# Two state-space chains that start one piece of the output projection later, in a Hymba-style decoder step on one core

## The chip, the cores and the metric

The kernel runs on one core of a Trainium2 chip. The metric is the device time of one execution in microseconds (us); lower is better. Engine names: PE is TensorE (matmuls), DVE VectorE, ACT ScalarE, POOL GpSimd, SP SyncE, which here only issues transfers.

## The reference

One inference step of one layer: sliding-window attention and a Mamba-2 state-space mixer side by side, an output projection, a squared-ReLU MLP. There are 1024 prompt tokens with 16 meta tokens ahead of them, and 32 sample tokens of 8 running sequences. The part that matters here, cut:

```python
def ssd_scan(x, dt, a, bm, cm, h0, chunk):            # chunks of 128 tokens, 8 heads
    ...
    decay = jnp.exp(jnp.where(causal, seg, -jnp.inf))
    g = jnp.einsum('bcthn,bcshn->bctsh', ch, bh) * decay
    y_diag = jnp.einsum('bctsh,bcshp->bcthp', g, xdt)
    s_chunk = jnp.einsum('bclhn,bclh,bclhp->bchpn', bh, to_end, xdt)
    ...
    def step(h, inp):                                 # the state goes from chunk to chunk
        s_c, tot_c = inp
        return h * tot_c[:, :, None, None] + s_c, h
    ...
    y_off = jnp.einsum('bclhn,bchpn->bclhp', ch, h_in) * jnp.exp(acum)[..., None]

def mix_and_mlp(h, ao, so, attn_out_g, w_out, norm2_g, w_up, w_down):
    mix = jnp.concatenate([rmsnorm(ao, attn_out_g), so], axis=-1)
    h = h + mix @ w_out
    u = jax.nn.relu(rmsnorm(h, norm2_g) @ w_up)
    return h + (u * u) @ w_down
```

## The kernel before, in words

The tokens are cut into nine state-space tiles: tile 0 has the 32 sample tokens and the 16 meta tokens, tiles 1 to 8 have 128 prompt tokens each. In the stage of this text two kinds of work share the engines.

The first is the attention half of the output projection, `wout_stream`. It has 24 pieces, one for an output block m of 128 rows and a token chunk ch: (0,0), (0,1), (1,0), (1,1), (0,2), (1,2), and then (m,0), (m,1), (m,2) for m from 2 to 7. A piece loads its rows of x (`hb<-in_xm`, L1013, two pieces ahead, four buffers), runs 12 matmuls into a bank g of three (288 or 384 columns, each product as three matmuls of high and low parts), adds the bank on DVE (`hb<-hb,g`, L1027) and stores the sum (`hd<-hb`, L1028, on SP).

The second is the state-space work, a chain for each tile, `mixer(i)`, which runs `ssd(i)` and then `gate(i)`; a generator whose `yield`s cut it into portions. Portion by portion, with the names of the tiles:

- PE transposes the tile's x (`s<-cs,xs`, L1081) and B (`s<-cs,bc`, L1083) and forms C·B (`s<-bc`); ACT scales x (L1087) and copies B (`Bt`, L1095); DVE makes `xd` (L1092) and `Gm` (L1097), POOL `xw` (L1094).
- PE makes the exponents of the decay in two halves (`s<-R,L`), ACT turns each into `Mt` (L1106, then L1107), DVE multiplies by `Gm` (L1108).
- After two more portions: `y<-Mt,xd`, the state's new part `s<-xw,Bt`, the state `hn` (POOL L1121 scales the last tile's, DVE L1126 adds; tile 0's is a plain ACT copy, L1128), and for tiles from 1 on `f<-bc,hn`; DVE adds the parts up (L1135 to L1138).
- Tile 0 goes on with four sample-state steps, `sample_state(j)`: each loads two tiles of 512 KB through SP (`st`, L1160, and `sT`, L1162), multiplies `sT` (`s<-sT,bc`), transposes the result (L1189), scales `st` on ACT (L1199), adds `s<-Bm,xS` to it on DVE (L1203) and stores it.
- `gate(i)` loads `zt` (L1212) and norms and splits the tile's output for the second half of the projection.

The banks of PSUM named s are a ring of three, shared by all chains; y and f have one each. `factors(i)` loads the decay factors `eA` (L967, two transfers) two slots ahead of the chain. `exponents` writes `R` and `L` for four tiles together.

`interleave` sets the order in which the program is written: slot by slot, first the chains that are due join, each live chain gives one portion, and then the stream gives one piece.

```python
            while chains and (chains[0][0] <= slot or not (more or live)):
                live.append(chains.pop(0)[1])
            live = [g for g in live if next(g, 1) is None]
            if more:
                more = next(gemms, 1) is None
            slot += 1
```

The slots are `round(2.25 * i)`, with 12 for tile 5: 0, 2, 4, 7, 9, 12, 14, 16, 18 for the tiles 0 to 8. From the written order the framework's scheduler makes the order on each engine, so that an instruction can stand some places away from where it is written; on each engine, SP's queue too, instructions then start in that order.

Of the kernel before, what the change touches and what calls it, by code (L numbers as in the profile page):

```python
# [20 lines left out]
NT = 9  # L21
# [167 lines left out]
def body(ctx: ExitStack, tc: tile.TileContext, xT, xm, win, wdt, wo, wu, wd, ck, cv, sc, st, sT, vec, consts,  # L189
# [5 lines left out]
    def pool(name, bufs=1, **kw):  # L195
        return tc.tile_pool(name=name, bufs=bufs, reuse_waits="tile", **kw)
# [13 lines left out]
    def gps():  # L210
        return psg.tile([128, 512], F32, name="g", tag="g", bufs=3)
# [32 lines left out]
    class Ahead:  # L244
# [9 lines left out]
        def next(self):  # L254
            while self.fns and len(self.got) <= self.n:
                self.more()
            return self.got.pop(0)

    def gemm(ps, w, act, k0=0):

        halves = isinstance(w[0], list)
        nk = 8 if halves else w[0].shape[1]
        for k in range(nk):
            for n, (a, b) in enumerate(((0, 0), (0, 1), (1, 0))):
                mm(ps, w[a][k // 4][:, k % 4, :] if halves else w[a][:, k, :], act[b][(k0 + k) // 4][:, (k0 + k) % 4, :], k == 0 and n == 0, k == nk - 1 and n == 2)

    def interleave(gemms, chains):

        gemms, chains, slot, live = iter(gemms), sorted(chains, key=lambda x: x[0]), 0, []
        more = True  # L270
        while more or live or chains:
# [6 lines that stand above are left out]
# [682 lines left out]
    def factors(i):  # L960

        M = TOK[i][1]
        z = "0" if i == 0 else ""
        eA = sp.tile([128, 4, M], F32, name="eA", tag="eA" + z, bufs=1 if i == 0 else 3)
        for hh in range(2):
            src = ed[8 * i:8 * i + 8, 0:M].rearrange("(j q) t -> q j t", q=2)[hh]
            SP.dma_start(out=eA[HALF[hh]], in_=src.unsqueeze(0).broadcast_to([64, 4, M]))  # L967
        EA[i] = eA
        yield
# [9 lines left out]
    def load_kept(m, ch, wk):  # L979

        c0, cw = CM[ch]
        hb = wk.tile([128, 384], F32, name="hb", tag="hb", bufs=4)[:, :cw]
        SP.dma_start(out=hb, in_=hd[:, m, c0:c0 + cw])
        return hb

    def mixer_half(m, ch, w, hb, wk, eng, tag="s2"):

        c0, cw = CM[ch]
        ps = gps()
        gemm(ps[:, :cw], w, X[ch], 4)  # L990
        DVE.tensor_tensor(out=hb, in0=hb, in1=ps[:, :cw], op=ALU.add)
        if m == 0:
            ACT.activation(out=sq[ch], in_=hb, func=AF.Square)
        else:
            s2 = wk.tile([128, 384], F32, name="s2", tag=tag, bufs=1 if tag == "s2" else 4)
            ACT.activation(out=s2[:, :cw], in_=hb, func=AF.Square)
            eng.tensor_tensor(out=sq[ch], in0=sq[ch], in1=s2[:, :cw], op=ALU.add)

    def gained(m, out, x):

        ACT.activation(out=out, in_=x, func=AF.Copy, scale=vec[:, V_G2 + m:V_G2 + m + 1])
# [3 lines left out]
    def wout_stream():  # L1005

        ws, hbs = {}, []
        order = [(0, 0), (0, 1), (1, 0), (1, 1), (0, 2), (1, 2)] + [(m, ch) for m in range(2, 8) for ch in range(3)]

        def load_x(m, ch):  # L1010
            c0, cw = CM[ch]
            hb = sp.tile([128, 384], F32, name="hb", tag="hb", bufs=4)[:, :cw]
            SP.dma_start(out=hb, in_=xm[:, 8 * c0 + m * cw:8 * c0 + (m + 1) * cw])  # L1013
            hbs.append(hb)

        load_x(*order[0])
        load_x(*order[1])
        for n, (m, ch) in enumerate(order):
            c0, cw = CM[ch]
            if m not in ws:  # L1020
                ws[m] = weights.next()
            if n + 2 < len(order):
                load_x(*order[n + 2])
            hb = hbs.pop(0)
            ps = gps()
            gemm(ps[:, :cw], ws[m], X[ch])
            DVE.tensor_tensor(out=hb, in0=hb, in1=ps[:, :cw], op=ALU.add)  # L1027
            SP.dma_start(out=hd[:, m, c0:c0 + cw], in_=hb)  # L1028
            yield
        acta_s.close()  # L1030
        opb = act_s.enter_context(pool("opb", side="right"))

        ha = xn["ha"] = opb.tile([128, 8, TM], F32, name="ha")
        c2 = CM[2][0]
        first = [load_kept(0, ch, sp) for ch in range(2)]
        SP.dma_start(out=ha[:, 1], in_=hd[:, 1])
        SP.dma_start(out=ha[:, 2], in_=hd[:, 2])
        SP.dma_start(out=ha[:, 0, c2:], in_=hd[:, 0, c2:])
        for m in range(3, 8):
            SP.dma_start(out=ha[:, m], in_=hd[:, m])  # L1040
        sq01 = opb.tile([128, CM[2][0]], F32, name="sq01")
        sq.update({ch: sq01[:, CM[ch][0]:CM[ch + 1][0]] for ch in range(2)})
        pieces = [(m, ch) for m in range(8) for ch in range(2)]
        weights.n = 3
        for m, ch in pieces:
            c0, cw = CM[ch]
            if ch == 0:
                w = weights.next()
            hb = ha[:, m, c0:c0 + cw] if m else first[ch]
            mixer_half(m, ch, w, hb, sp, DVE if m > 2 else POOL)  # L1050
            if m == 0:
                SP.dma_start(out=he[:, m, c0:c0 + cw], in_=hb)
                gained(m, ha[:, m, c0:c0 + cw], hb)
            elif ch == 0 and m > 1:
                SP.dma_start(out=he[:, m - 1, 0:c2], in_=ha[:, m - 1, 0:c2])
            elif ch == 1 and m > 3:
                gained(m - 3, ha[:, m - 3, 0:c2], ha[:, m - 3, 0:c2])
            yield
        SP.dma_start(out=he[:, 7, 0:c2], in_=ha[:, 7, 0:c2])
        for m in (5, 6, 7):  # L1060
            gained(m, ha[:, m, 0:c2], ha[:, m, 0:c2])
# [163 lines left out]
    def decays(i):  # L1225
        exponents(*((48, 32, slice(0, 1)) if i == 0 else (128, 128, slice(i, i + 4))))
        yield

    def mixer(i):
        if i == 0:  # L1230
            yield from decays(i)
        yield from ssd(i)

    interleave(wout_stream(), [(max(0, (12 if i == 5 else round(2.25 * i)) - 2), factors(i)) for i in range(NT)] + [(12 if i == 5 else round(2.25 * i), mixer(i)) for i in range(NT)] +
               [(1, decays(1)), (10, decays(5))])
    SP.dma_start(out=hp, in_=hs[8])
    w3.close()
# [656 lines left out]
```

## Time and profile before

| | us |
|---|---|
| median of 3 runs | 1120.18 |
| the three runs | 1119.13 to 1121.18 |
| the profiled execution | 1119.52 |
| its span, first to last instruction | 1117.8 |
| mean granted clock of TensorE over the span | 0.997 of full speed |
| the stage of the two kinds of work | about 290 to 394 of the span |

A row of the timeline gives start, duration, engine, line, operation, output<-input, shape and count; several like instructions in a row are merged, and what stands in brackets is the idle time before and what ended it. A row of the waits gives who waited for whom, the sum in us, how often, and the longest. A row of windows gives the window, its length, the busy time of each engine shown, TensorE's granted clock, the share of the transfer engines and GB/s. All matmuls are issued from L199. (i) behind a name in the text is the tile's number, counted from 0.

### The profile page before, as it was taken

To read this page: it belongs to the slowest core of one execution; us is meant where nothing else is said; L and a number is where in the kernel's file an instruction comes from. 1 tells how busy PE (TensorE), PEld (TensorE's weight loads), DVE (VectorE), ACT (ScalarE), POOL (GpSimd) and SP (SyncE) were. 2 spreads that over 40 slices of the span, in tenths; PEclk is the share of its full clock that TensorE was granted. 3 is DMA by queue.
4 is the path that set the end of the run, shared out by engine and by line. 5 is a ranking of instruction groups with operands and counts; after the bars stand their busy time and mean duration, and the time that the engine had idled before them with its cause. 6 is when DMAs were issued, how large, how long until landed. Compare 5 with 4: busy or idle time off the path is not lost.

```text
span 1117.8 us, 21656 instructions
## 1 busy us (share of the span) xinstructions
PE 1101.4 (99%) x8312; PEld 1063.4 (95%) x8312; DVE 832.7 (75%) x1652; ACT 557.3 (50%) x1188; POOL 215.4 (19%) x296
## 2 busy tenths in 40 slices
PE   9999999999999999999999999999999999999997
PEld 8989988989888899999999999999999999999997
DVE  6646888985879968988877777676599657768483
ACT  8312467575655558744444444444434343546461
POOL 0442365564245432200000000000000000000001
PEclk9999999999999999999999999999999999999999
DMA  8231110111497486656643434425989663465273
GB/s 285 73 99 39 40 37 22 39 59 53 140 273 235 142 290 223 207 183 229 200 150 139 179 106 157 161 100 203 392 291 311 190 182 90 127 197 161 80 230 110
DMA packets 89259, 179.53 MB, mean 161 GB/s; under 512 B 11488, under 2 KB 37704, under 8 KB 87108
## 3 DMA queue, kind: packets, MB, share of 16 engines
q1 hardware_dynamic: 82372, 143.76, 41.2%
q0 software_dynamic: 6080, 33.48, 7.5%
q8 instruction: 65, 1.06, 0.4%
q10 hardware_dynamic: 704, 0.92, 0.2%
q14 instruction: 38, 0.31, 0.1%
HBM read 127.36 MB, written 50.76 MB: 159 GB/s over the span
## 4 chain that ended last, share of the span: by engine, by line
PE 78%; DVE 10%; issue 4%; ACT 3%; POOL 3%; DMA 2%; POOLq 0%; SPq 0%; DVEq 0%; ACTq 0%
PE g L199 44%; PE b L199 18%; PE c L199 9%; PE s L199 3%; PE o L199 1%; DVE bc L522 1%; DMA wdr<-in_wd 1%; POOL wlo L231 1%; PE y L199 1%; DVE Sd L1639 1%; PE pt L199 1%; DMA wraw<-in_win 1%; DVE p L675 1%; DMA u<-b 1%; DVE ts L1653 0%
## 5 line engine op out<-in xcount | busy, mean ns | idle before, releaser
L199 PE MATMUL g<-acth,whi 128*128 128x384 f32 (+2 forms) x528 | 161.4, 331 | 0.2 <-DVE qT L452 0.2
L199 PE MATMUL g<-acth,wlo 128*128 128x384 f32 (+2 forms) x528 | 159.8, 327 | 0.0
L199 PE MATMUL g<-actl,whi 128*128 128x384 f32 (+2 forms) x432 | 140.4, 325 | 0.0
L1652 ACT CAST ts<-tr 128x528 fp32r<-128x528 f32 x92 | 58.2, 632 | 119.1 <-PE b L199 97.4
L1653 DVE TENSOR_TENSOR ts<-tr,ts 128x528 fp32r<-128x528 f32 x92 | 65.1, 708 | 56.6 <-ACT ts L1652 56.1
L199 PEld LDWEIGHTS g<-acth,whi 128*128 128x128 f32 x528 | 97.0, 188 | 2.1 <-issue 1.2
L199 PEld LDWEIGHTS g<-acth,wlo 128*128 128x128 f32 x528 | 97.6, 189 | 0.5 <-issue 0.2
L199 PEld LDWEIGHTS g<-actl,whi 128*128 128x128 f32 x432 | 81.4, 188 | 0.2
L318 POOL TENSOR_TENSOR rs<-rs,nhalf 128x3 f32<-128x3 f32 x9 | 9.6, 1066 | 338.7 <-DVE rs L317 338.7
L1368 ACT COPY s<-g 128x264 f32<-128x264 f32 x90 | 34.0, 377 | 63.7 <-PE g L199 61.7
L231 POOL TENSOR_TENSOR wlo<-wraw,whi 128x256 fp32r<-128x256 f32 x56 | 48.9, 903 | 10.9 <-ACT whi L228 10.6
L1441 POOL DMA_DIRECT2D u<-u x16 | 8.5, 532 | 177.2 <-ACT u L1384 146.7
L1373 DVE TENSOR_TENSOR u<-b,s 128x264 f32<-128x264 f32 x64 | 27.5, 430 | 19.7 <-PE b L199 10.1
L1378 ACT ACTIVATE u<-u 128x528 f32<-128x528 f32 x42 | 27.1, 646 | 26.6 <-DVE u L1377 26.6
L199 PE MATMUL b<-ts,w7y 128*128 128x264 f32 x279 | 39.3, 285 | 0.0
L199 PE MATMUL g<-ts,whi 128*128 128x264 f32 x279 | 38.9, 284 | 0.0
L199 PE MATMUL g<-ts,w7y 128*128 128x264 f32 x279 | 38.9, 283 | 0.0
L199 PE MATMUL b<-ts,whi 128*128 128x264 f32 x279 | 38.9, 284 | 0.0
L199 PE MATMUL g<-ts,wlo 128*128 128x264 f32 x270 | 38.0, 285 | 0.0
L199 PE MATMUL b<-ts,wlo 128*128 128x264 f32 x270 | 37.3, 283 | 0.0
L199 PEld LDWEIGHTS b<-ts,w7y 128*128 128x128 f32 x279 | 36.1, 188 | 0.0
L199 PEld LDWEIGHTS b<-ts,whi 128*128 128x128 f32 x279 | 36.0, 188 | 0.0
(588 smaller groups left out, 3430.1 us busy)
## 6 DMA issues: line engine op xcount, KB each, us to landing
tr<-u SPq DMA_DIRECT2D x92, 264.0 KB, 3.0
wraw<-in_wu SPq DMA_DIRECT2D x38, 512.0 KB, 4.0
wdr<-in_wd SPq DMA_DIRECT2D x68, 256.0 KB, 3.6
u<-t POOLq DMA_DIRECT2D x16, 1056.0 KB, 5.7
wraw<-in_win SPq DMA_DIRECT2D x16, 512.0 KB, 3.7
u<-u POOLq DMA_DIRECT2D x10, 792.0 KB, 3.6
wraw<-in_wo SPq DMA_DIRECT2D x24, 256.0 KB, 2.8
h<-he SPq DMA_DIRECT2D x16, 264.0 KB, 5.3
```

The lines of the kernel that those rows point to most:

```text
L199: PE.matmul(out, lhsT=a, rhs=b, start=start, stop=stop, skip_group_check=on)
L231: eng.tensor_tensor(out=lo[:, n], in0=raw[:, n], in1=f(hi[:, n]), op=ALU.subtract)
L318: POOL.tensor_tensor(out=out, in0=out, in1=nhalf[:out.shape[0], :w], op=ALU.pow)
L522: DVE.scalar_tensor_tensor(out=acc, in0=cb[:, j:j + CL], scalar=cw_(j), in1=acc, op0=ALU.mult, op1=ALU.add)
L675: DVE.tensor_tensor_reduce(out=s_out[:, 0:W], in0=ps, in1=mask, scale=-scale, scalar=nsink, op0=ALU.add, op1=ALU.min, accum_out=nm)
L1368: ACT.copy(out=s[:, c], in_=ps[c][:, :TQ])
L1373: DVE.tensor_tensor(out=out[:, c], in0=ps[c][:, :TQ], in1=s[:, c], op=ALU.add)
L1378: ACT.activation(out=x, in_=x, func=AF.Square)
L1441: POOL.dma_start(out=u7[p][:, 4 + a:7], in_=u[:, a:3])
L1639: tt(out=s, in0=s, in1=r, op=ALU.subtract)
L1652: ACT.copy(out=t[:, 0], in_=x)
L1653: DVE.tensor_tensor(out=t[:, 1], in0=x, in1=f(t[:, 0]), op=ALU.subtract)
```

## The change

The slot of each chain comes from a small function, which gives 3 for tile 1 (before 2), 5 for tile 2 (before 4), and the same as before for all others. The loads of the decay factors of those two tiles start one slot later as well (1 and 3 for 0 and 2).

```diff
-    interleave(wout_stream(), [(max(0, (12 if i == 5 else round(2.25 * i)) - 2), factors(i)) for i in range(NT)] + [(12 if i == 5 else round(2.25 * i), mixer(i)) for i in range(NT)] +
+    def at_slot(i):
+        return {1: 3, 2: 5, 5: 12}.get(i, round(2.25 * i))
+
+    interleave(wout_stream(), [(max(0, at_slot(i) - 2), factors(i)) for i in range(NT)] + [(at_slot(i), mixer(i)) for i in range(NT)] +
                [(1, decays(1)), (10, decays(5))])
```

The number of instructions is the same; the order on the engines differs from the first pieces of the stream to the end of the stage. Three places follow. Numbers behind a name tell buffers apart, and differ between the two kernels.

SP's queue around the first sample-state step, before. hb_3257, hb_3259, hb_3271, hb_3323, hb_3381 and hb_3409 belong to the pieces (0,0), (0,1), (1,0), (1,1), (0,2) and (1,2):

```order
L1028 DMA hd_3227<-hb_3259 128x384
L1160 DMA st_3490<-in_st 128x1024
L1013 DMA hb_3381<-in_xm 128x384
L1028 DMA hd_3227<-hb_3271 128x288
L1013 DMA hb_3409<-in_xm 128x384
L1028 DMA hd_3227<-hb_3323 128x384
L1162 DMA sT_3492<-in_sT 128x1024
```

And after; here the same six pieces are hb_3254, hb_3256, hb_3268, hb_3323, hb_3356 and hb_3398, and hb_3449 is piece (2,0):

```order
L1028 DMA hd_3227<-hb_3268 128x288
L1013 DMA hb_3398<-in_xm 128x384
L1028 DMA hd_3227<-hb_3323 128x384
L1160 DMA st_3468<-in_st 128x1024
L1013 DMA hb_3449<-in_xm 128x288
L1028 DMA hd_3227<-hb_3356 128x384
L1162 DMA sT_3470<-in_sT 128x1024
```

The issue of sT stood behind the store of piece (1,1), and now stands behind the store of piece (0,2), one piece later.

DVE's queue at the same place, before (Mt_3398 is tile 1's; g_3383 and g_3411 are the banks of the pieces (1,0) and (1,1)):

```order
L1097 TENSOR_TENSOR Gm_3371<-s_3355,cs_66 128x256
L1027 TENSOR_TENSOR hb_3271<-hb_3271,g_3383 128x288
L1108 TENSOR_TENSOR Mt_3398<-Mt_3398,Gm_3371 128x512 x2
L1027 TENSOR_TENSOR hb_3323<-hb_3323,g_3411 128x384
L1136 TENSOR_TENSOR xs0_3236<-xs0_3236,y_3426 128x192
```

And after (Mt_3438 is tile 1's, xd_3489 is tile 2's; g_3451 is the bank of piece (0,2)):

```order
L1146 TENSOR_TENSOR xS_3430<-xw_3300,xS_3430 32x512
L1146 TENSOR_TENSOR BS_3431<-Bt_3301,BS_3431 32x256
L1108 TENSOR_TENSOR Mt_3438<-Mt_3438,Gm_3393 128x512 x2
L1027 TENSOR_TENSOR hb_3356<-hb_3356,g_3451 128x384
L1092 TENSOR_TENSOR xd_3489<-s_3475,dt_111 128x512
```

The sum of piece (0,2), which SP's store waits for, now stands directly behind the Mt pair of tile 1. On ACT the four steps that make this pair stand behind tile 0's copy, after:

```order
L1145 CAST xS_3430<-xw_3300 32x512
L1128 COPY hn_3425<-s_3424 128x512
L1106 ACTIVATE Mt_3438<-s_3439 128x512
L1106 ACTIVATE Mt_3438<-s_3444 128x512
L1107 ACTIVATE Mt_3438<-Mt_3438 128x512 x2
```

Before, they stood ahead of that copy.

PE at the first sample-state step, as one piece of the difference (- before, + after; the sT row is the step; acth_3099 belongs to piece (1,2), acth_3091 to piece (2,0); y, f and s<-xw,Bt are tile 1's, s<-R,L tile 2's):

```order
 L199 MATMUL g<-acth_3099,wlo 128x384
-L199 MATMUL s<-sT,bc_3237 32x128 x8
+L199 MATMUL y<-Mt,xd 64x128 x8
+L199 MATMUL f<-bc,hn 128x128 x4
 L199 MATMUL g<-acth_3091,whi 128x288
 L199 MATMUL g<-actl_3093,whi 128x288
-L199 MATMUL g<-acth_3091,whi 128x288 x2
+L199 MATMUL g<-acth_3091,whi 128x288
+L199 MATMUL s<-sT,bc_3237 32x128 x8
+L199 MATMUL s<-xw,Bt 128x256 x2
+L199 MATMUL s<-R,L 128x512 x2
+L199 MATMUL g<-acth_3091,whi 128x288
```

The multiplication by sT stood between the pieces (1,2) and (2,0). It now stands behind the first three matmuls of piece (2,0), and tile 1's s<-xw,Bt and tile 2's two decay matmuls stand behind it.

## The prediction

> **What bounds the kernel now.** I read the busy times and the chain of the page first, then the busy times of the stage that the change touches, then TensorE's waits there, and the timelines of the engines last.
>
> ```profile
> span 1117.8 us, 21656 instructions
> PE 1101.4 (99%) x8312; PEld 1063.4 (95%) x8312; DVE 832.7 (75%) x1652; ACT 557.3 (50%) x1188; POOL 215.4 (19%) x296
> ...
> PE 78%; DVE 10%; issue 4%; ACT 3%; POOL 3%; DMA 2%; POOLq 0%; SPq 0%; DVEq 0%; ACTq 0%
> ...
> 290.00:394.00 104.00, 101.09 (x746) 87.30 (x745) 93.31 (x206) 62.07 (x156) 46.44 (x47) 0.98 0.69 212
> ```
>
> TensorE is busy for 99% of the span. The last row is the stage with the output projection and the state-space chains, about 290 to 394 us: TensorE 101.1 of 104 us, VectorE 93.3. The edit neither adds nor removes an instruction, so TensorE's work stays. What can move is its idle time there, 104 - 101.1 = 2.9 us, and the time it spends at a lower clock.
>
> ```profile
> PE y L199 <- DVE Mt L1108: 0.8, 2, 0.5
> PE s L1081 <- ACT Mt L1106: 0.6, 1, 0.6
> PE s L1081 <- DVE L L953: 0.3, 1, 0.3
> PE s L1083 <- ACT Mt L1106: 0.3, 1, 0.3
> ```
>
> ```profile
> 296.00:297.00 1.00, 0.68 (x4) 1.00 0.90 307
> 297.00:298.00 1.00, 0.43 (x4) 1.00 0.97 289
> 298.00:299.00 1.00, 0.67 (x7) 1.00 0.52 160
> 299.00:300.00 1.00, 1.00 (x6) 0.50 0.02 5
> 300.00:301.00 1.00, 0.92 (x4) 0.50 0.00 0
> 301.00:302.00 1.00, 1.00 (x5) 0.50 0.52 155
> 302.00:303.00 1.00, 1.00 (x6) 0.80 0.36 106
> ```
>
> The first fence is TensorE's named waits in the stage: few and short. The second is TensorE alone in steps of 1 us (length, busy, granted clock, DMA). In 296 to 299 it is idle for 0.32 + 0.57 + 0.33 = 1.22 us, in several gaps, and the clock then stands at 0.50 for three steps and 0.80 in the next: 3 x 0.5 + 0.2 = 1.7 us of full-speed work lost.
>
> **The change, part by part.** Below, (i) stands for state-space tile i, counted from 0.
>
> *The head, up to 300 us.* TensorE's rows down to the matmuls of tile 1's B and C (s<-bc) stand in the same order in both kernels, and so do the rows that release them. I leave the gaps of 296 to 299 and the low clock as they are: 0. Behind them, the two decay matmuls of tile 1 (s<-R,L) move behind the next product piece. The step 300 to 301 has 0.08 us idle in front of the first of them; it can go: -0.1, between -0.1 and 0.
>
> *The transfer of sT, the term that decides.* The first sample-state step needs the 512 KB tile sT. In the changed order its issue on SP stands behind the store hd<-hb of piece (0,2); that store waits for VectorE's sum L1027, which now stands behind the two Mt products L1108 of tile 1; those wait for ScalarE's four Mt steps, which stand behind the copy hn<-s (L1128), which waits for TensorE's s<-xw,Bt of tile 0. So sT now hangs on TensorE's own progress. I measure both paths from the start of y<-Mt,xd(0), at 303.88 in the trace, so the time of that start cancels.
>
> ```profile
> 303.88 0.67 PE L199 MATMUL y<-Mt,xd 48*64 48x48 f32 x16
> 304.48 1.13 PE L199 MATMUL s<-xw,Bt 16*128 16x256 f32 x4
> 305.53 0.66 PE L1081 MATMUL s<-cs,xs 128*128 128x128 f32 x4
> ...
> 306.61 0.42 PE L199 MATMUL g<-acth,whi 128*128 128x384 f32 x1
> ...
> 308.87 1.09 PE L199 MATMUL y<-Mt,xd 128*64 128x128 f32 x16
> 309.90 1.13 PE L199 MATMUL s<-xw,Bt 128*128 128x256 f32 x4
> 310.86 1.05 PE L199 MATMUL f<-bc,hn 128*128 128x128 f32 x8
> 311.67 0.71 PE L199 MATMUL s<-R,L 128*128 128x512 f32 x2
> 312.22 0.34 PE L199 MATMUL g<-acth,wlo 128*128 128x384 f32 x1
> ...
> 314.40 0.64 PE L199 MATMUL s<-sT,bc 128*32 128x128 f32 x16
> 314.98 0.40 PE L199 MATMUL g<-acth,whi 128*128 128x288 f32 x1
> ...
> 315.35 0.43 PE L199 MATMUL g<-acth,whi 128*128 128x288 f32 x2
> ...
> 316.81 0.72 PE L199 MATMUL s<-Bm,xS 96*128 96x512 f32 x2
> ```
>
> ```profile
> 305.64 0.59 ACT L1128 COPY hn<-s 128x512 f32<-128x512 f32 x1 [1.61 <-PE s L199]
> ...
> 312.19 1.09 ACT L1106 ACTIVATE Mt<-s 128x512 f32<-128x512 f32 x2 [2.58 <-PE s L199]
> 313.16 1.15 ACT L1107 ACTIVATE Mt<-Mt 128x512 f32<-128x512 f32 x2
> ```
>
> ```profile
> 314.59 1.29 DVE L1108 TENSOR_TENSOR Mt<-Mt,Gm 128x512 f32<-128x512 f32 x2
> 315.79 0.55 DVE L1027 TENSOR_TENSOR hb<-hb,g 128x384 f32<-128x384 f32 x1
> ```
>
> ```profile
> 305.57 0.40 SPq L1028 DMA_DIRECT2D hd<-hb  x1
> 306.01 0.45 SPq L1162 DMA_DIRECT2D sT<-in_sT  x1
> ```
>
> ```profile
> DMA to landing us min/median/max: 5.0/5.1/5.6
> ```
>
> ```profile
> DMA to landing us min/median/max: 2.7/4.2/5.0
> ```
>
> The path of the transfer: 303.88 to the start of hn, 1.76; hn 0.59; from the L1106 pair to the L1107 pair 0.97; the L1107 pair 1.15; one L1108 behind it 1.29/2 = 0.65; L1027 0.55; from SP's store to SP's sT issue 0.44; landing 5.1 (the first landing row, of the four sT transfers). Sum 11.2 us.
>
> TensorE's path to s<-sT in the new order: y and s<-xw,Bt of tile 0, 1.65 (303.88 to 305.53); two decay matmuls 0.55 (311.67 to 312.22); piece (0,2) 2.26 (306.61 to 308.87); transposes and s<-bc of tile 2, 1.08 (305.53 to 306.61); piece (1,2) 2.26; y(1) 1.03; f(1) 0.81; three matmuls of piece (2,0), 0.5 (two take 0.37 from 314.98). Sum 10.1 us.
>
> So TensorE would wait 11.2 - 10.1 = 1.1 us for sT, with s<-xw,Bt(1), both decay matmuls of tile 2 and the rest of piece (2,0) queued behind it. Before there is room: issued at 306.01, landed about 311.1, used at 314.40. With the slowest sT landing, 5.6, the wait is 1.6. The second landing row is tile st, of the same size: 2.7 at best would put sT in place 1.3 us ahead of its use, 0. I take the median of sT itself; ends 0 and 1.6.
>
> *Banks freed later, right behind it.* The ring s has three banks. In the new order the two banks of s<-Bm,xS are wanted next by tile 3's s<-cs,bc and tile 2's s<-xw,Bt, after VectorE's st sums have read them.
>
> ```profile
> 318.46 2.45 ACT L1199 ACTIVATE st<-st,e 128x128 f32<-128x128 f32 x8 [2.34 <-DVE e L1197]
> ```
>
> ```profile
> 319.77 0.69 DVE L1203 TENSOR_TENSOR st<-st,s 128x512 f32<-128x512 f32 x1 [0.48 <-ACT st L1199]
> ```
>
> Before, the first bank comes free at 319.77 + 0.69 = 320.46, 3.65 after Bm starts at 316.81. In the new order the two Bm matmuls, twelve of the product, the transposes of xs and three y matmuls stand between: 0.65 + 2.26 + 0.5 + 0.2 = 3.6. That is even, but VectorE has the L1108 pair of tile 2 (1.29) on this stretch too, of which a part comes ahead of the st sums: a wait between 0 and 0.7, I take 0.3. A second place of the kind follows at tile 4's first decay matmul; both bounds together 0 to 1.2.
>
> *Later waits.* VectorE's L953, and L1108 twice, hold TensorE for 0.3 + 0.8 = 1.1 us further on. With TensorE 1.3 later these may partly go. VectorE waits for the same delayed matmuls and is 90% busy in the stage, so it is late too: I take -0.2, between -1.1 (all gone) and +1.1 (as many new ones). Behind the stage the rows are the same but for a few, 0.
>
> Every other moved step (loads of eA one piece later, POOL's xw and hn products one place apart, the copies of wraw) ends before its reader on the paths above: SP issues eA ahead of sT, and POOL is busy 46 of 104 us.
>
> Sum: -0.1 + 1.1 + 0.3 - 0.2 = +1.1 us. The profiled execution took 1119.52 us, 0.7 below the median of the runs shown (1120.18, from 1119.13 to 1121.18); on its scale this is 1120.6, and on that of the median 1120.18 + 1.1 = 1121.3.
>
> **The rivals.**
> N, on time: sT lands by the lower row, or the later waits take the lag up. Then -0.1 + 0 to 0.3 - 0.2, about 0: 1120.2. For it speaks that one landing of 3.9 would be enough, against it that all four sT landings take 5.0 or more.
>
> S1, slower: the wait for sT brings the clock down as the gaps before 299 did. Price 1.7: +2.8, 1123.0. It decides once the idle time in some 3 us passes what 296 to 299 had, 1.22. Against it:
>
> ```profile
> 487.00:488.00 1.00, 0.00 (x0) 1.00 0.96 255
> ```
>
> A whole step without TensorE, and the clock stays at 1.00. [...]
>
> S2, slower: bank waits at their upper end, 0.7, at all four sample-state steps instead of 0.3 once: -0.1 + 1.1 + 2.8 - 0.2 = +3.6, 1123.8. For it: the four steps repeat the pattern, and VectorE has under 11 us idle in the stage. Against it: from tile 3 on the two orders run nearly alike.
>
> G, faster: the gaps of 296 to 299 no longer lower the clock (-1.7), sT is on time (0), and the later waits go (-1.1): -2.9, 1117.3. It decides only with the clock and at least half of the waits; the waits alone give -1.2. Against it: TensorE's rows up to 300 are the same. [...]
>
> **How the numbers follow.** Chances: forecast 0.42 (own range 1120.4 to 1122.6), N 0.20, S1 0.13, S2 0.12, G 0.13. About 0.2%, 2.2 us, is what a measurement of this kernel can tell from no change: 1117.9 to 1122.4. Faster is G, 0.13. Slower is S1 and S2 and 0.04 of the forecast's upper end, 0.29. Same is the rest, 0.58. The range, 1118.2 to 1123.8, leaves out G and half of S2, 0.19.
>
> **What would show it.** Right: TensorE has a wait of about 1 us before s<-sT near 313.5, released by a transfer, and SP's sT issue comes near 309 instead of 306; short waits of s<-cs,bc for VectorE's st near 322; the low clock stays at 299 to 302.6. Wrong: no wait at s<-sT, because sT lands in under 4 us or SP issues it earlier; a second stretch of low clock behind it; or full clock at 300.

## The result, and the profile after

| | kernel before | changed kernel |
|---|---|---|
| median | 1120.09 us (8 runs) | 1125.51 us (8 runs) |
| lowest to highest | 1118.61 to 1121.94 | 1123.31 to 1128.72 |
| the profiled execution | 1119.52 | 1126.11 |
| its span | 1117.8 | 1124.3 |

The ratio of the times is 1.0049 (here and in the table below the ratio is worked out on its own, and can differ by up to 0.1% from the quotient of the two medians), with a 95% interval from 1.0035 to 1.0064. The change is slower by 5.4 us; the prediction said 1121.3, 1.1 slower, with 1123.8 as the upper end. A later series of runs (e0 below) gave 1124.35 against 1120.08, ratio 1.0037 (1.0025 to 1.0049).

The page of the changed kernel: its span, the busy times, and the shares of the chain that ended last.

```profile
span 1124.3 us, 21664 instructions
PE 1103.9 (98%) x8312; PEld 1066.3 (95%) x8312; DVE 832.9 (74%) x1652; ACT 556.8 (50%) x1188; POOL 216.1 (19%) x296
...
PE 78%; DVE 8%; issue 4%; DMA 3%; ACT 3%; POOL 3%; POOLq 0%; SPq 0%; ACTq 0%; DVEq 0%
```

TensorE has the same 8312 matmuls and is busy 2.5 us longer (1103.9 for 1101.4). The same matmuls take longer where the granted clock is lower (a pair of 128x512 decay matmuls takes 0.71 us at full clock, in the prediction's rows at 311.67, and 1.17 at half clock, at 318.40 in the changed kernel), so this part of the loss is clock. The other 4.0 of the 6.5 us of span are idle time of TensorE (20.4 for 16.4). The window of the stage, with the columns of the prediction's row of it (PE, PEld, DVE, ACT, POOL, clock, DMA share, GB/s):

```profile
290.00:394.00 104.00, 98.73 (x728) 85.86 (x726) 89.78 (x193) 60.81 (x154) 46.06 (x45) 0.97 0.69 205
```

In the same 104 us TensorE works 98.73 for 101.09, and VectorE 89.78 for 93.31: both got less done. The waits of TensorE in the changed kernel, those of the stage first and then two behind it:

```profile
PE s L199 <- DMA sT<-in_sT: 2.5, 1, 2.5
PE y L199 <- DVE Mt L1108: 0.9, 2, 0.6
PE s L1083 <- ACT Mt L1106: 0.6, 1, 0.6
```

```profile
PE g L199 <- ACT s L1371: 2.2, 1, 2.2
PE g L199 <- ACT acth L1222: 0.9, 1, 0.9
```

In the kernel before, this one row stood in place of the last pair (line numbers behind 1231 are lower by 3 there), and no wait for acth:

```profile
PE g L199 <- ACT s L1368: 1.5, 1, 1.5
```

The wait for sT is 2.5 us where 1.1 was predicted. What made sT late stands in the timelines of VectorE, of GpSimd, of VectorE's first Mt product alone, and of SP (start, length, engine, line, what), and of TensorE last:

```profile
307.08 3.68 DVE L1108 TENSOR_TENSOR Mt<-Mt,Gm 128x512 f32<-128x512 f32 x2 [1.66 <-ACT Mt L1107]
310.68 0.54 DVE L1027 TENSOR_TENSOR hb<-hb,g 128x384 f32<-128x384 f32 x1
```

```profile
306.62 1.90 POOL L1171 TENSOR_TENSOR Bm<-BS,cs 96x1024 fp32r<-96x1024 f32 x1
308.48 1.74 POOL L241 TENSOR_TENSOR whi<-wraw,whi 128x512 fp32r<-128x512 f32 x1
```

```profile
307.08 1.99 DVE L1108 TENSOR_TENSOR Mt<-Mt,Gm 128x512 f32<-128x512 f32 x1 [1.66 <-ACT Mt L1107]
```

```profile
305.69 0.33 SPq L1013 DMA_DIRECT2D hb<-in_xm  x1
311.25 0.33 SPq L1028 DMA_DIRECT2D hd<-hb  x1
311.67 0.38 SPq L1162 DMA_DIRECT2D sT<-in_sT  x1
```

```profile
315.88 1.08 PE L199 MATMUL s<-sT,bc 128*32 128x128 f32 x16 [2.48 <-DMA sT<-in_sT]
```

The chain of the prediction is there, link by link: SP has nothing to do from 306 to 311.25, because its next row is the store of piece (0,2), which waits for VectorE's sum at 310.68, which stands behind the two Mt products. But the two products take 3.68 us, not 1.29. GpSimd's Bm product ends at 308.52 and its whi product at 310.22; the first Mt product (1.99, the third fence shows it alone) ended at 307.08 + 1.99 = 309.07 and the pair at 310.76, each 0.54 to 0.55 behind the end of GpSimd's instruction. So it looks as if each Mt product did its work only when GpSimd's was over; e7 below tests that. GpSimd's side is longer there as well: its whi product takes 1.74 us here, and 1.27 in the kernel before (at 310.35).

Then the clock. TensorE alone in steps of 1 us (length, busy, granted clock, DMA share, GB/s):

```profile
314.00:315.00 1.00, 0.00 (x0) 1.00 0.96 319
315.00:316.00 1.00, 0.12 (x4) 0.86 0.70 135
316.00:317.00 1.00, 1.00 (x17) 0.50 0.95 242
317.00:318.00 1.00, 1.00 (x3) 0.50 1.02 356
318.00:319.00 1.00, 1.00 (x4) 0.50 1.00 370
319.00:320.00 1.00, 1.00 (x7) 0.93 1.01 367
```

Behind the wait the clock is at 0.50 for 3.4 us, which costs up to 1.7 us of work. By the rows it is 1.4: from 315.88 to 319.41 TensorE does s<-sT, s<-xw,Bt(1) and the two decay matmuls of tile 2, 3.53 us for what takes 0.58 + 0.96 + 0.55 = 2.09 in the prediction's rows. The prediction's rival S1 came true. A third stretch of this kind stands behind the longer wait at 491 (0.61, 0.50, 0.50, 0.68 in the four steps from 493); before, the 1.47 us there had no such follower.

The last new wait, 0.9 us, has its cause in ScalarE's queue:

```profile
397.62 0.62 ACT L240 CAST wlo<-wraw 128x512 fp32r<-128x512 f32 x1 [1.79 <-PE g L199]
398.14 0.81 ACT L1222 CAST acth<-xs 128x128 fp32r<-128x128 f32 x2
```

```profile
398.49 0.40 PE L199 MATMUL g<-acth,whi 128*128 128x288 f32 x1 [0.91 <-ACT acth L1222]
```

The cast of wlo waits for a buffer that TensorE frees with its last piece; tile 0's copy acth, which TensorE's next piece needs, now stands behind it. Before, that copy stood ahead of the cast:

```profile
392.04 0.28 ACT L1222 CAST acth<-xs 128x128 fp32r<-128x128 f32 x1
394.30 0.62 ACT L240 CAST wlo<-wraw 128x512 fp32r<-128x512 f32 x1 [1.98 <-PE g L199]
```

The sum for the profiled pair: the waits give 2.48 for sT, 0.91 for acth and 0.73 for the wait at 491 (2.20 for 1.47), together 4.1, where TensorE's idle time grew by 4.0. The two new low stretches cost 1.4 us and, at 493, 1.5 (24 products from 493.36 on take 4.48 us, and 3.01 before), together 2.9, where its busy time grew by 2.5. The wait at 491 was 1.4 in a second profile of the changed kernel (e0 below), with no low clock behind it, so its 0.73 us and its low stretch are not shown to belong to the change. y(0) starts 0.69 earlier (303.19 for 303.88), but that is order more than time, since both decay matmuls of tile 1 stood ahead of it and now stand behind it.

### The profile page after: what moved, and what is told of

It is laid out like the page before. It is cut to its first block, busy times and chain, and to the rows that moved or that the text cites. A ratio compares the mean times of both kernels' runs of the same rounds, so it can differ in the third digit from the quotient of the medians.

```text
span 1124.3 us, 21664 instructions
## 1 busy us (share of the span) xinstructions
PE 1103.9 (98%) x8312; PEld 1066.3 (95%) x8312; DVE 832.9 (74%) x1652; ACT 556.8 (50%) x1188; POOL 216.1 (19%) x296
## 4 chain that ended last, share of the span: by engine, by line
PE 78%; DVE 8%; issue 4%; DMA 3%; ACT 3%; POOL 3%; POOLq 0%; SPq 0%; ACTq 0%; DVEq 0%
PE g L199 44%; PE b L199 17%; PE c L199 9%; PE s L199 3%; PE o L199 1%; DVE bc L522 1%; DMA wdr<-in_wd 1%; PE y L199 1%; POOL wlo L231 1%; DVE Sd L1642 1%; PE pt L199 1%; DMA wraw<-in_win 1%; DMA u<-b 1%; DVE ts L1656 0%; ACT acth L405 0%
```

## The experiments

Times in us; "before" is the median of the kernel before in the runs beside it. From here on, "the swap" is sT loaded ahead of st, "Bm on ScalarE" the first Bm product made there, "acth on VectorE" tile 0's copy made there, "banks" tile 0's decay matmuls in the banks y and f.

| run | kernel | median | before | ratio (95% interval) |
|---|---|---|---|---|
| e0_after_again | changed kernel | 1124.35 | 1120.08 | 1.0037 (1.0025 to 1.0049) |
| e1_tile1 | tile 1 alone moved | 1123.82 | 1120.25 | 1.0028 (1.0017 to 1.0040) |
| e2_tile2 | tile 2 alone moved | 1120.28 | 1120.25 | 1.0002 (0.9991 to 1.0013) |
| e3_after_swap | changed, swap | 1121.02 | 1120.25 | 1.0012 (1.0000 to 1.0023) |
| e4_before_swap | before, swap | 1120.52 | 1120.08 | 1.0003 (0.9992 to 1.0014) |
| e7_bmact | changed, Bm on ScalarE | 1121.26 | 1120.25 | 1.0008 (0.9992 to 1.0023) |
| e13_before_bmact | before, Bm on ScalarE | 1119.91 | 1119.42 | 0.9998 (0.9987 to 1.0009) |
| e15_after_both | changed, swap, Bm on ScalarE | 1118.95 | 1119.42 | 0.9988 (0.9976 to 1.0001) |
| e11_before_banks | before, banks | 1120.19 | 1120.08 | 1.0003 (0.9993 to 1.0013) |
| e12_after_banks | changed, swap, banks | 1120.58 | 1120.08 | 1.0005 (0.9993 to 1.0017) |
| e17_before_banks_fill | before, banks, filler matmuls | 1120.42 | 1119.42 | 0.9999 (0.9988 to 1.0011) |
| e14_tile1_bmact | tile 1 alone, Bm on ScalarE | 1122.19 | 1119.42 | 1.0018 (1.0006 to 1.0030) |
| e18_after_acth | changed, acth on VectorE | 1122.54 | 1119.90 | 1.0020 (1.0011 to 1.0029) |
| e19_after_three | changed, all three mends | 1118.67 | 1119.90 | 0.9993 (0.9982 to 1.0003) |
| e20_tile1_three | tile 1 alone, all three mends | 1121.15 | 1119.90 | 1.0010 (1.0000 to 1.0020) |

**Which tile.** Two kernels move one of the two tiles:

```diff
-        return {1: 3, 2: 5, 5: 12}.get(i, round(2.25 * i))
+        return {1: 3, 5: 12}.get(i, round(2.25 * i))      # e1
+        return {2: 5, 5: 12}.get(i, round(2.25 * i))      # e2
```

> Only tile 1 starts one piece later (slot 3); tile 2 keeps slot 4. SP's issue of sT then stands ahead of the store of piece (0,2). Theory T (the loss is the issue of sT behind that store, 2.5 us of waiting, and the low clock that follows it, 1.7 us): sT is issued near 306, TensorE waits under 0.5 us before the first s<-sT, no low clock at 315 to 320, time within 2 us of before (1118.5 to 1122). Rival O (a later chain costs by itself, wherever sT stands): half or more of the loss stays, 1122.5 to 1125, without a wait for sT.

> Only tile 2 starts one piece later (slot 5); tile 1 keeps slot 2. SP's queue up to sT is that of the kernel before. Theory T: sT is issued near 306, no wait before the first s<-sT, no second stretch of low clock, 1118.5 to 1121.5. Rival O: slower by 2 us or more through later waits, 1122 to 1125.

Tile 2 alone is without effect, as theory T said. Tile 1 alone costs 3.2 us in the ratio, and there theory T failed: sT was issued at 306.1, no wait for it, and yet the loss is there. The profiled run, at 1121.32, is one of the fastest of its twelve. Its longest waits (the second one behind the stage, near 397):

```profile
PE s L199 <- DVE Gm L1097: 1.2, 1, 1.2
...
PE g L199 <- ACT acth L1222: 1.4, 1, 1.4
```

And VectorE has two long Mt pairs there, beside products of GpSimd (Bm and xw, then whi and wlo):

```profile
307.08 3.44 DVE L1108 TENSOR_TENSOR Mt<-Mt,Gm 128x512 f32<-128x512 f32 x2
...
311.43 2.37 DVE L1108 TENSOR_TENSOR Mt<-Mt,Gm 128x512 f32<-128x512 f32 x2
```

So moving tile 1 does two things, whatever sT does: it puts Mt pairs beside GpSimd's products, and it puts acth behind the cast.

**The order of the two loads.**

```diff
         st = sp.tile([128, 8, 128], F32, name="st", tag="st", bufs=2)
-        SP.dma_start(out=st, in_=st_in[j])
         sT = sp.tile([128, 8, 128], F32, name="sT", tag="sT", bufs=1)
         SP.dma_start(out=sT, in_=sT_in[j])
+        SP.dma_start(out=st, in_=st_in[j])
```

> The changed kernel with the two loads of a sample-state step in the other order, sT ahead of st, so that sT takes the place of st on SP, ahead of the store of piece (0,2). Theory T: sT is issued near 304.5 and there before TensorE reaches s<-sT; the wait of 2.5 us and the low clock of 315.7 to 319.1 go, together 4.2 us; 1121.3 if the waits near 398 and 492 stay, down to 1119 if they go too. Rival O: the chains are late whatever sT does; the time stays at 1124 to 1126 and the idle time turns up at other tiles' waits. Also to be seen: the Mt pair L1108 still takes over 3 us beside POOL's Bm and whi products.

> The kernel before with the two loads of a sample-state step in the other order. Only SP's queue differs. Theory T: sT was in place 3.3 us ahead of its use already, so the order of the loads changes nothing there: 1119 to 1121.5, the same as before. If it is faster by 1 us or more, the gain of the same edit in the changed kernel isn't (only) the wait for sT.

In the changed kernel this takes back most of the loss: 1121.02, 0.12% over before by the ratio (0.00 to 0.23), against 0.37 to 0.49% without it. In the kernel before it does nothing. In the profile of e3, sT is issued at 304.5, the Mt pair takes 4.25 us, and the wait is shorter, though not gone, with no low clock behind it:

```profile
310.05 0.64 PE L199 MATMUL s<-sT,bc 128*32 128x128 f32 x16 [1.01 <-DMA sT<-in_sT]
```

The wait stays at 1.0 because with sT planned earlier the multiplication stands earlier too, right behind piece (1,2) (at 310.05, for 315.88), and because this execution had full clock at 299 (y(0) starts at 301.38, for 303.19). The wait for acth, 0.9, stays.

**What makes the Mt pair long.**

```diff
-            POOL.tensor_tensor(out=Bm[0], in0=f(Bt[:, g, :])..., in1=c("seqm", 96)..., op=ALU.mult)
+            for b in range(8 if j == 0 else 0): ACT.activation(out=Bm[0][:, b, :], in_=f(Bt[:, g, :]), func=AF.Copy, scale=c("seqm", 96)[:, b:b + 1])
+            if j: POOL.tensor_tensor(out=Bm[0], ...)
```

> The changed kernel with the first Bm product made by eight ScalarE copies with a scale, in place of one GpSimd product; SP, TensorE and the head of VectorE's queue keep their order up to sT. Theory P (the Mt pair L1108 takes 3.68 us in place of 1.3 because VectorE's products of two SBUF operands wait for GpSimd's running product): the pair takes 1.3 to 2.0 us, sT is issued near 309.5 in place of 311.67, TensorE's wait before s<-sT is 0.2 to 1.0 us, and the low clock behind it does not come: 2 + 1.7 us back, 1121 to 1122.5. Rival Q (the pair is long for a reason of its own, or the wait is decided by the transfer's landing): the pair stays over 3 us or the wait over 2 us; 1124 to 1126.5.

> The kernel before with the first Bm product on ScalarE (eight copies with a scale) in place of GpSimd; TensorE's, VectorE's and SP's orders stay in the stage. A control for the same edit in the changed kernel. Theory P (the edit helps only where VectorE's Mt pair stands beside that product): in the kernel before, the pair ran at 302 to 304, ahead of it, so nothing is to be gained: 1119 to 1121. Rival: ScalarE's products take load off GpSimd in any order, and this kernel too is 1 us or more faster: 1117.5 to 1119.

Theory P is right about the pair. In e7:

```profile
305.22 1.29 DVE L1108 TENSOR_TENSOR Mt<-Mt,Gm 128x512 f32<-128x512 f32 x2
306.43 0.55 DVE L1027 TENSOR_TENSOR hb<-hb,g 128x384 f32<-128x384 f32 x1
```

```profile
307.43 0.38 SPq L1162 DMA_DIRECT2D sT<-in_sT  x1
```

```profile
301.33 0.67 PE L199 MATMUL y<-Mt,xd 48*64 48x48 f32 x16
...
313.08 0.65 PE L199 MATMUL s<-sT,bc 128*32 128x128 f32 x16 [1.57 <-DMA sT<-in_sT]
```

GpSimd has nothing to do while the pair runs (it is idle from 304.80 to 307.66), and the pair takes 1.29. From y(0) to SP's issue it is 307.43 - 301.33 = 6.10 us, and TensorE's path to s<-sT is 313.08 - 1.57 - 301.33 = 10.18. The prediction had 6.1 and 10.1: with the pair at its own length its sum holds. The landing is 5.65, at its upper end of 5.6, and so the wait 1.57, at its upper end of 1.6; I had expected 0.2 to 1.0 here. The clock stays at 1.00 behind it. The time is 1121.26, as theory P said, and the same edit in the kernel before is without effect (e13). The profiled execution took 1118.13, 3.1 under that median; the mean clock of the twelve runs goes from 0.994 to 0.999, so one profile at full clock does not stand for all of them.

> The changed kernel with both mends, sT loaded ahead of st and the first Bm product on ScalarE. Theory T with P: the wait for sT is under 1 us, the Mt pair under 2 us, and only the waits near 398 stay: 1119.5 to 1121, about what either mend gives alone (1121.0 and 1121.3), since both take away the same wait. Rival (two losses of their own): the gains add up, 1117 or less.

With both mends the wait for sT is gone, the pair is 1.29, and the median is 1118.95, 0.5 under the kernel before, and the ratio, 0.9988, is lower than either gives alone (1.0012 and 1.0008). The interval reaches from 0.24% faster to no difference. The gains do not add up in full (that would be 1117), nor are they the same gain only: each alone leaves 1.0 or 1.6 us of waiting for sT.

**The clock.**

> The changed kernel once more, for a second profiled execution and more times beside the same runs of the kernel before. Theory C (TensorE's clock is watched in windows of a fixed length that run on whatever the kernel does, so that the same idle gaps cost 1.7 us in one execution and nothing in another): the wait of some 2.5 us before s<-sT, the Mt pair L1108 of 3.5 to 3.8 us and the wait for ScalarE's acth near 398 are all there again; the low clock stretches need not be the three of the first profile (near 299, 316 and 493), each that comes is 3.4 us long and costs 1.7, and the span goes with their number. Rival: the same gaps give the same stretches each time. Time 1124 to 1127.

Theory C is borne out by this second profile: it has full clock at 299 and at 493, and a double stretch behind a wait of 3.04 us for sT:

```profile
313.00:314.00 1.00, 0.00 (x0) 0.95 1.35 222
314.00:315.00 1.00, 0.51 (x12) 0.50 0.90 169
...
319.00:320.00 1.00, 1.00 (x6) 0.50 0.98 308
320.00:321.00 1.00, 1.00 (x6) 0.64 0.15 50
```

Between 277 and 508 us of the 17 profiles a low stretch is 3.41 us long (in ten of them) or 6.83 (e0); six have none there. Two executions have three such stretches, and their starts lie a whole multiple of 3.413 us apart: 298.66, 315.73 and 493.22 in the changed kernel's first profile, 299.06, 316.12 and 493.61 in e18, 5 and 52 times in both. In e0 the low clock starts at 313.90, which counted back in the same steps is 300.25: in two executions of one kernel the steps lie 1.6 us apart. So I take the clock to be set for a window of 3.413 us at a time, whatever instruction stands at its edge. With such windows laid over the profiles, TensorE's idle time in each, worked out from its busy time; the first two groups have all windows with 1.27 us or more in that part of the 17 profiles, and one with 0.59. In the profile before and the changed kernel's first, no other window of 1.27 or more lies ahead of the last 20 us of the span:

```
idle us in a window of 3.413 us, and the clock in the next window

0.50 next:  2.45 e0 310.5-313.9    2.33 after 312.3-315.7  2.27 e11 296.4-299.8
            2.20 e18 312.7-316.1   2.06 after 489.8-493.2  1.94 e18 490.2-493.6
            1.88 e12 485.2-488.6   1.62 e14 392.9-396.3    1.44 e19 425.2-428.6
            0.59 e0 313.9-317.3 (itself at 0.50)
1.00 next:  1.57 e7 310.7-314.1    1.47 before 486.7-490.1 1.45 e4 486.6-490.0
            1.42 e0 491.4-494.8    1.42 e1 394.4-397.8     1.27 e4 343.3-346.7

in 294 to 301:
0.50 next:  1.22 before, 1.10 after, 1.21 e1, 1.00 e2, 1.21 e4, 1.21 e18, 1.21 e19
            (all windows that begin at 295.2 to 295.6)
1.00 next:  0.89 e3, 0.88 e13, 0.88 e15, 0.88 e20 (begin at 294.5 to 294.7),
            1.26 e12 (begins at 297.4), 0.74 e7, 0.73 e0, 0.76 e14 (begin at 297)
```

From 1.62 us of idle time on, the clock always halved in the next window; at 1.57 and below it did not, with two exceptions: 1.44, where TensorE's first work behind the gap was six matmuls of one column (c<-ones,sq, 128x1), and 0.59 in e0, the second half of the double stretch, where the window was at half clock already. No run takes either apart. In 295 to 299, where the work is transposes and small matmuls, 1.00 to 1.22 were enough; why less idle time was enough there is not shown.

Two kernels change the gaps themselves. e11 takes away the waits for banks at 296 to 299:

```diff
-            pd = ptile()
+            pd = ptile(("y", "f")[g] if i == 0 else "s")
```

> The kernel before, with the two decay matmuls of tile 0 (s<-R,L) in the banks y and f, which nothing uses until then, in place of two banks of the ring s; TensorE's order stays. Theory C2 (the gaps of 296 to 299, transposes of tile 1 that wait for ScalarE's L1106 to read those two banks, are what lowers the clock at 299): the waits s<-ACT Mt L1106 of 0.6 and 0.3 us go, and the low clock at 299 with them; faster by 0.9, and by up to 2.6 where the low clock came; 1117.5 to 1119.5. Rival: TensorE waits as long a little later, for VectorE's L and R of tile 1 (ready near 298.7 to 300), and the clock falls all the same: 1119.5 to 1121.

> The changed kernel with sT loaded ahead of st and with tile 0's decay matmuls in the banks y and f: the two edits together. Theory T with C2: 0.9 to 2.6 us less than with the loads alone (1121.0): 1118.5 to 1120.5, the same as the kernel before or a little faster, and no faster than the kernel before with the banks alone. Rival: TensorE, earlier by the 0.9 us, waits that much longer for sT (1.0 us with the loads alone): 1120.5 to 1121.5.

The rival came true in e11. The two waits went, and TensorE stood in one piece instead, for VectorE's L, with the low clock behind it:

```profile
299.79 0.76 PE L199 MATMUL s<-R,L 128*128 128x512 f32 x1 [2.27 <-DVE L L953]
```

e12 lost the gain to a new wait of 1.3 us for VectorE's L1027, and its ratio lies within the interval of e3.

e17 fills e11's wait with ten repeated products of tile 1:

```diff
-        for g in range(2):
+        for g in list(range(2)) * (6 if i == 1 else 1):
             mm(pb[:M, 256 + M * g:256 + M * g + M], B_[:, g, :], C_[:, g, :], True, True)
```

> The kernel before with tile 0's decay matmuls in the banks y and f, where TensorE then waits 2.27 us at a stretch for VectorE's L (297.5 to 299.8) with low clock behind it; and here the two small products C B of tile 1 ahead of that wait are done six times over, ten matmuls more, some 1.8 us of work in the wait. Theory C (the clock falls after a window with some 1.7 us or more without matmuls): the wait shrinks to about 0.5 us, no low clock behind it; more work, and 0.5 to 1.7 us less time than with the banks alone (1120.2): 1118.5 to 1119.7. Rival (the low clock has nothing to do with the idle time, or the ten matmuls delay the chain): 1120 to 1122.

The clock did what theory C says. TensorE alone from 299 on, in e11:

```profile
299.00:300.00 1.00, 0.21 (x1) 0.90 0.00 0
300.00:301.00 1.00, 1.00 (x4) 0.50 0.02 7
```

and in e17:

```profile
299.00:300.00 1.00, 0.97 (x7) 1.00 0.00 0
300.00:301.00 1.00, 1.00 (x6) 1.00 0.11 38
```

and the mean clock of its twelve runs lies at 0.998 to 0.999, where that of the kernel before, beside them, goes from 0.995 to 0.999. But the time did not fall (ratio 0.9999). y(0) starts 1.1 us earlier than in the kernel before (302.78 for 303.88), the first piece of the projection's second half only 0.57 (393.53 for 394.10), and at 484 the lead is gone. So of the full clock at 299 nothing is left at the end of e17. I take it that VectorE, 90% busy in the stage, sets the pace behind it; that is argued, not shown, and e17 also moves two banks and adds ten matmuls.

It does not follow that a low window costs nothing. Over 309 runs on record, each set against the mean of its own kernel and series, a run whose mean clock is lower by 0.0015 (one window of 3.413 us at half clock in 1118 us) took 1.0 us longer, with a standard error of 0.1; in the 128 runs of the kernel before alone it is 0.8. This counts low windows wherever they lie. The two profiles of the changed kernel agree: each has two low windows ahead of 398, at 299 and 316 in the first, both from the wait for sT on in e0. In e0 y(0) is 2.1 us earlier than in the first and the wait for sT 0.56 longer, and TensorE's next piece starts at 398.49 in both: the rest of the lead, 1.5 us, is gone with one low window more behind the wait. That fits a window at 299 that costs about as much as one behind the wait; one pair of profiles does not prove it.

**What else tile 1 costs.**

> Only tile 1 one piece later (1123.8), and the first Bm product on ScalarE. The question is what makes tile 1 alone slow without a wait for sT. Theory P2 (the Mt pairs of tiles 1 and 2, 3.44 and 2.37 us beside GpSimd's products, make VectorE late and with it the later tiles): the pair takes 1.3 to 1.8 us, and the waits for Gm (1.2) and rsb (0.6) go: 1121 to 1122.5. Rival K (the order of the later stage: ScalarE's acth behind its cast of wlo near 396, 1.4 us, and the banks near 331): both waits stay, 1123 to 1125.

The pairs are shorter (2.13, with GpSimd's xw still beside it, and 1.29), the wait for Gm is gone, those for acth (1.4) and rsb (0.6) stay, and one for sT (1.1) is new, since this execution had full clock at 299 and TensorE came earlier. 1122.2: within P2's range, but with K's waits; the Mt pairs are about a third of tile 1's loss by the ratios (1.0028 and 1.0018), with intervals that overlap.

```diff
-        ACT.copy(out=hi, in_=y)
+        (ACT.copy if i else DVE.tensor_copy)(out=hi, in_=y)
```

> The changed kernel with one copy moved to another engine: tile 0's part of acth (L1222, 128x128), which stands behind the cast of wlo (L240) on ScalarE's queue there, is made by VectorE. Theory K (0.9 us near 398 in every version with tile 1 a piece later is that order on ScalarE: the cast waits for a buffer that TensorE frees, and TensorE's next piece waits for the copy behind it): the wait g<-ACT acth L1222 of 0.9 goes, the wait for sT and the long Mt pair stay; 0.9 less than the changed kernel (1124.4 to 1125.5): 1123 to 1125. Rival: another wait of about the same length takes its place within the next 10 us, or near 450 to 492.

> The changed kernel with the three mends: sT loaded ahead of st, the first Bm product on ScalarE, tile 0's part of acth on VectorE. Theory T, P and K together: no wait for sT, Mt pair under 2 us, no wait for acth near 398; up to 0.9 less than with the first two (1118.95): 1117.8 to 1119.5, faster than the kernel before by 0.5 to 2 us. Rival: the time lies with VectorE and with the later stage, and takes the 0.9 back: 1119 to 1120.

> Only tile 1 one piece later, with the same three mends. With the Bm product alone mended it was at 1122.2, 2.4 us over the kernel before, with waits for acth (1.4), sT (1.1), rsb (0.6). Theory T, P and K: these three are the loss; 1119.5 to 1120.5. Rival (moving tile 1 without tile 2 costs by the banks and by VectorE's order near 330 to 357): 1121.5 to 1123.

In e18 the wait for acth is gone, and nothing takes its place there; the wait for sT (2.2), the pair (3.69) and the three low stretches are those of the changed kernel:

```profile
395.42 0.21 DVE L1222 CAST acth<-xs 128x128 fp32r<-128x128 f32 x1
```

Its ratio is 1.0020, 0.17 to 0.29% (1.9 to 3.2 us) under the changed kernel in its two series; 0.9 us was expected, which the intervals of this run and e0 allow. The same copy on VectorE in the kernel before was not run, so it is not shown that all of this gain belongs to the change. e19, with all three, has none of the three waits; its ratio of 0.9993 (0.9982 to 1.0003) does not stand clear of the kernel before, and is no lower than that of e15 (0.9988), so the third mend added nothing that can be told from noise. e20, tile 1 alone with the three, is at 1121.15, between the two expectations: short waits for t1s, rsb, sqy and dg, 0.3 to 0.7 each, are left. What moves them was not tried.

## Why the prediction was wrong, point by point

- *What bounds the kernel*: right. TensorE's work is the same, and all of the loss is its idle time and its clock.
- *The head, -0.1*: about right. y(0) came 0.69 earlier, but both decay matmuls of tile 1 now stand behind it. At equal work the gain is 0.25: tile 2's transposes start at 307.54, behind one more piece of 2.26, and before at 305.53.
- *The transfer of sT, +1.1*: this is the step that failed, by one term in it. The path was right in each link, and e7 reproduces it to 0.1 us (6.10 and 10.18 for 6.1 and 10.1). The term "L1027 behind one L1108, 1.29/2" was taken from a pair that ran beside an idle GpSimd. In the new place Bm and whi run, and the pair took 3.68: SP issued sT 8.48 us behind y(0), not 6.1. The landing was 4.2, under my 5.1, and the wait 2.48. The text had dismissed GpSimd as "busy 46 of 104 us"; its instructions at that very place were in the order of the changed kernel, and the trace of before had the sign of the matter, a first Mt product of 1.05 us beside GpSimd's xw, where the second, alone, takes 0.69:

```profile
302.65 1.05 DVE L1108 TENSOR_TENSOR Mt<-Mt,Gm 128x512 f32<-128x512 f32 x1
304.06 0.69 DVE L1108 TENSOR_TENSOR Mt<-Mt,Gm 128x512 f32<-128x512 f32 x1 [0.35 <-ACT Mt L1107]
```

- *Banks freed later, +0.3*: no wait of this kind over 0.2 us in the stage. Too high, and of no weight.
- *Later waits, -0.2, and "behind the stage 0"*: the second step that failed. In the stage, the wait for L953 went, the two for L1108 stayed (0.9), and one of 0.6 for L1106 is new: +0.4 in place of -0.2. Behind it, the order of ScalarE's queue near 397 had changed, with a wait of 0.91 that is there in every version with tile 1 a piece later and acth on ScalarE (0.9 to 1.4). I had compared the orders around the sample-state step and not at the stage's end, so "behind the stage 0" was a term put at nothing without a reason.
- *Rival S1, 13 in 100*: it was the case. Its condition, more than 1.22 us of idle time in some 3 us, is not the right one (1.57 stayed without effect in e7); its price of 1.7 is near, 1.4 by the rows. Its chance was my estimate: I weighed it against a single gap of 1.47 that had no effect, with a wait of 1.1 in mind; at 2.48 it would have been likely. Its time, 1123.0, with the wait at its measured size and the wait for acth, is 1120.18 + 2.48 + 1.4 + 0.9 - 0.25 = 1124.7, near the measured 1124.4 and 1125.5.
- *Rival G*: its low clock at 299 came in one execution of the changed kernel (0.50 in the first profile) and not in the other (1.00 in e0). That it would be worth 1.7 us is not borne out: e17, with a mean clock of 0.998 or more in all runs, is no faster, and over all runs a low window goes with 1.0 us.
- *What would show it*: the wait released by a transfer, the late issue of sT and the second low stretch were all there; the issue at 311.67, not 309, was the row that told it.

## What to carry to other kernels

A duration read from a trace holds beside the neighbours it had there: when an edit moves a VectorE product of two SBUF tensors, look up what GpSimd runs beside it in the new order, and where GpSimd's instruction starts first, take its end as the start of the product (here the pair took 3.68 us for 1.29, and each product ended 0.54 to 0.55 behind the end of a GpSimd instruction). A transfer whose issue stands behind a store on one queue inherits every delay of the engine that feeds the store (here sT was issued 8.48 us behind y(0), not 6.1); the load that is needed first goes first (here the order of two lines took back some 3 to 4 us of the changed kernel's loss). Compare the orders of all queues at the end of the changed stage as well, where an operand for the next stage can end up behind an instruction that waits for the last one.

## What the hardware showed that I had not expected

- Two VectorE products of two SBUF operands took 1.29 us beside an idle GpSimd and 3.0 to 4.3 us beside its Bm product and the one behind it (3.68, 3.44, 4.25, 4.26, 3.02, 3.69 in six profiles), and in each of the six the pair ended 0.54 to 0.57 us behind the end of a GpSimd instruction.
- The clock was low for 3.41 us at a time, or for 6.83, and not at the same places each time: the same kernel had its low stretches at 299, 316 and 493 in one execution, whole multiples of 3.413 us apart, and at 314 alone, twice as long, in another. Behind all eight windows with 1.62 us or more without matmuls the next was at half clock. Over 309 runs, one such stretch went with 1.0 us of time.
- Ten more matmuls in a wait of 2.27 us kept the mean clock at 0.998 or more in all of twelve runs, and the time did not move (ratio 0.9999, 0.9988 to 1.0011).
